# Four blocks of the attention output product, instead of two, computed between the heads up to their last depth block

## The chip, the cores and the metric

One core of one Trainium2 chip. The metric is the device time of the kernel in microseconds (us). The kernel before takes 2140.32 us, the median of three runs (2138.83 to 2141.16).

## What is computed

A two-layer trunk over 1024 positions of width 1024, all in float32: a gated linear recurrence and a squared-ReLU MLP, then chunked band attention with a learned relative bias and a second squared-ReLU MLP. The change lies in the attention layer and its output product:

```python
q = rmsnorm((rmsnorm(h, b_norm) @ b_w_q).reshape(bsz, s, N_HEADS, HEAD_DIM), b_q_norm)
o = chunk_band_attention(q, k_pad, v_pad, rel_bias)   # 16 heads of 64, chunks of 64, 8 chunks to the left
h = h + o @ b_w_o                                     # the output product
h = h + sqrelu_mlp(rmsnorm(h, mlp_norm), w_up, w_down)
```

## The kernel before

Activations lie transposed: 8 depth blocks of 128 features by 1024 positions, cut into two halves of 512 positions (`h` = 0, 1). To keep float32 accuracy every operand of a product is split into a high and a low part (an ACTIVATE makes the high part, a subtraction on VectorE or GpSimd the low part), and one 128x128 block by 512 columns takes three matmuls (`mm`, L334 to L336). Here such a triple is called a step. Weights come in pairs of raw 128x512 tiles, 256 KB each, and in the attention they are split at L297 (ScalarE) and L300 (VectorE) into tiles that the products read.

**The attention stage** (L1697 to L1720, in the trace from about 945 to 1455 us) is laid out by a planner written in the kernel (`Plan`, `Flag`, `Sema`): it simulates the engines with cost formulas and so fixes the order of the instructions on each queue. Two streams are interleaved.

- The *units* are the attention proper: 16 heads, two per depth block t, each in four units of 256 queries, so 64 units. A unit scores (L1556, L1557; VectorE adds the bias and takes the minimum at L1560, ScalarE the exponential at L1569, GpSimd scales at L1573), transposes the probabilities (L1581), splits them (L1589, L1591), and multiplies by the values into a bank `po` (L1608, L1609). After the second unit of a half, `leave` takes the result out (L1618, L1620). For t < 6 it is stored to DRAM (`od`); for t = 6 and 7 it is split at once by `halves` (L1632, L1634).
- The *filling* (`filling`, L1677) is dense matrix work: for t = 0 to 7 the projections of keys, queries and values (48 steps per t, 384 in all), and then `wo_steps`. This computes JP = 2 blocks of 128 output features of the output product over the first seven depth blocks only (the last one, t = 7, is not there yet): 2 blocks x 2 halves x 7 steps = 28 steps. The stored outputs are brought back during the last value projection and the first blocks (`reload`, L1638), six tiles per half, and split on ScalarE and GpSimd (L1632, L1634).

A unit may begin when the count of filling steps has reached its `due` value, and the filling may run at most SLACK = 14 steps past the next unit's due value. The due values are spread evenly over the filling:

```python
total = 8 * 6 * NF + 2 * JP * (NF - 1)        # 412 steps
cost = [1.0 if n.h else FR for n in units]    # FR = 0.9, sum 60.8
due = [START]                                 # START = 48
for c in cost:
    due.append(due[-1] + (total - START) * c / sum(cost))
```

When a block's seven steps are done, `Out.first` (L853 to L858) loads the residual `x2d` into a tile of the pool `sp` (tag s, NS = 10 tiles), adds the bank to it on VectorE (L857) and keeps the sum. The planner counts the addition but not the load. `weight` (L1477) hands out the next weight and starts the split of the one after it; the list `later` (L266 to L271) sets the order: the projections' weights, the first JP blocks of w_o, a tile `wl7` with the last depth block of all eight output blocks, then the remaining blocks of w_o.

**After the planned stage** (L1723 on) the order is set by the tile framework's scheduler, which may also place such instructions earlier, inside the stage, when their buffers are free. For the JP blocks the last depth block is one step per half; L1729 adds it to the kept sum, and `Out.last` stores the result, adds its square to the norm (L381, L387) and, for each finished pair of blocks, calls `combine` (L876 to L898), 11 VectorE and 8 ScalarE instructions that make the seven operands of the MLP's first product. `up_first` loads the first MLP weights. `whole` (L908) computes the other six blocks, 24 matmuls per block and half, each followed by `first` and `last`. Then `up_begin` (L1070) starts the MLP.

All DMAs are issued on SyncE's queue, in order; an issue waits there until its tile is free.

Of the kernel before, what the change touches and what calls it, by code (L numbers as in the profile page):

```python
# [40 lines left out]
C_ISSUE = 0.55  # L41
C_MOVE = 2.4
DEFER = 3
JP = 2
SC = (2.5, 5.0)
AHEAD = 1
ET = mybir.EngineType
# [110 lines left out]
def tile_yoco_rglru_chunk_attention(  # L158
# [108 lines left out]
    for t in range(NF):  # L267
        later += [(w_kv[t], g_kv, pool), (w_q[t], g_q, pool), (w_kv[NF + t], g_kv, pool)]
    later += [(w_o[j], None, WOE) for j in range(JP)]
    later.append((w_o[:, :, NF - 1, :].rearrange("j p m -> p j m"), None, dve))  # L270
    later += [(w_o[j], None, dve) for j in range(JP, NF)]  # L271
    loading, ready = [], []
# [36 lines left out]
    def next_w(late=False):  # L309
        while len(ready) < (1 if late else 2) and fetched[0] + len(loading) > 0:  # L310
            if not loading:
                if fetched[0] == len(wlist):
                    break
                fetch()
            prep()
        while len(loading) < AHEAD and fetched[0] < len(wlist):
            fetch()
        return ready.pop(0)
# [1337 lines left out]
    def wo_steps():  # L1656
        for j0 in range(0, JP, 2):
            js = range(j0, min(j0 + 2, JP))
            ws = []
            for _ in js:  # L1660
                w = yield from weight()
                ws.append(w)
            for h in range(2):
                for j, w in zip(js, ws):
                    ps = bank("pj")
                    for k in range(NF - 1):
                        if (h, j) == (0, js[-1]) and j0 == 0 and k < NF - 2:
                            plan.start(units[0].reload(k, 1))
                        yield split_o[k, h]
                        mm(ps, wparts(w, k), OS[k][h], k == 0, k == NF - 2)  # L1670
                        plan.pe(3 * H2)
                        if k == NF - 2:
                            o3.first(ps, j, h)
                            plan.use("dve", c_dve(H2))
                        yield None

    def filling():  # L1677
        for t in range(NF):
            projs.append(Proj(t))
            n = 0  # L1680
            for y in projs[t].steps():
                if y is None:
                    n += 1
                    if t == NF - 1 and 0 <= n - 5 * NF - 2 < NF - 2:
                        plan.start(units[0].reload(n - 5 * NF - 2, 0))
                yield y
        yield from wo_steps()

    fill = filling()
    total = 8 * 6 * NF + 2 * JP * (NF - 1)  # L1690
    cost = [1.0 if n.h else FR for n in units]
# [31 lines left out]
    wl7 = next_w()  # L1723
    for j in range(JP):
        for h in range(2):
# [74 lines left out]
```

## Time and profile before

| | |
|---|---|
| median of 3 runs | 2140.32 us |
| the profiled execution | 2141.76 us, span of the trace 2140.0 us |
| TensorE busy | 2092.7 us (98%), 9768 matmuls |
| VectorE / ScalarE / GpSimd busy | 1544.4 / 1106.4 / 577.2 us |
| chain that ended last, by engine | TensorE 86%, VectorE 6%, ScalarE 3%, DMA 2% |

The ends of matmuls are modelled and overlap the next one, so that a busy TensorE tells only that it did not wait; the time from one start to the next tells its pace. A row of a timeline gives the start, the duration, the engine, the line, the operation, the tile written and those read, the shape and the count, and in square brackets the engine's idle time before it and what ended it.

### The profile page before, as it was taken

What the parts mean: (1) busy time and instruction counts of PE and PEld (TensorE: products, weight loads), DVE (VectorE), ACT (ScalarE), POOL (GpSimd) and SP (SyncE); (2) the same over time, 40 slices, a digit from 0 to 9 for tenths busy, and PEclk for the clock granted to TensorE, in tenths of its full rate; (3) what the DMA queues carried; (4) which work ended last, traced back from release to release, by engine and by line L of the source; (5) the groups of instructions that cost most, each with busy time, mean ns of one, the idle gap of its engine ahead of it and who ended that gap; (6) DMA issues with size and microseconds to landing.
All of it is one profiled execution on the core that took longest, in us unless ns stands there. A gap on an engine that the chain in (4) does not pass through costs nothing.

```text
span 2140.0 us, 29346 instructions
## 1 busy us (share of the span) xinstructions
PE 2092.7 (98%) x9768; PEld 1732.8 (81%) x9768; DVE 1544.4 (72%) x2602; ACT 1106.4 (52%) x1965; POOL 577.2 (27%) x511
## 2 busy tenths in 40 slices
PE   7999899999999999999999999989999999999999
PEld 5788787888888888887888888878778888888887
DVE  7767768877777776747777877767787777777843
ACT  5777645444434544546666666764443444444631
POOL 0123202333310000127666666650133332000000
PEclk8999999999999999999999999999999999999999
DMA  4111334544469784534323332343364444987732
GB/s 139 35 50 50 107 116 153 182 158 153 149 231 314 240 259 131 161 121 109 86 75 97 91 91 83 87 151 123 103 215 148 155 156 170 332 262 242 244 109 94
DMA packets 174296, 319.21 MB, mean 149 GB/s; under 512 B 20544, under 2 KB 22592, under 8 KB 174144
## 3 DMA queue, kind: packets, MB, share of 16 engines
q1 hardware_dynamic: 174144, 317.33, 45.8%
q8 instruction: 77, 1.26, 0.2%
q14 instruction: 75, 0.61, 0.1%
HBM read 219.73 MB, written 78.64 MB: 139 GB/s over the span
## 4 chain that ended last, share of the span: by engine, by line
PE 86%; DVE 6%; ACT 3%; DMA 2%; issue 2%; SPq 1%; POOL 0%; DVEq 0%; POOLq 0%; ACTq 0%
PE pj L334 11%; PE pj L335 11%; PE pj L336 11%; PE tp L334 6%; PE tp L336 6%; PE tp L335 6%; PE sc L336 4%; PE sc L335 4%; PE sc L334 4%; PE p L335 4%; PE p L334 3%; PE p L336 3%; PE tp L1581 2%; PE po L1609 2%; PE po L1608 1%
## 5 line engine op out<-in xcount | busy, mean ns | idle before, releaser
L334 PE MATMUL pj<-h,wh 128*128 128x512 f32 x1198 | 481.5, 402 | 4.9 <-DVE s L1116 3.6
L335 PE MATMUL pj<-l,wh 128*128 128x512 f32 x1198 | 468.0, 391 | 0.7 <-POOL l L1634 0.7
L336 PE MATMUL pj<-h,wl 128*128 128x512 f32 x1198 | 467.9, 391 | 0.2
L1035 ACT ACTIVATE wh<-raw 128x512 fp32r<-128x512 f32 x349 | 219.1, 629 | 317.5 <-PE po L335 68.9
L1036 DVE TENSOR_TENSOR wl<-raw,wh 128x512 fp32r<-128x512 f32 x349 | 269.8, 775 | 100.3 <-ACT wh L1035 96.5
L336 PEld LDWEIGHTS pj<-h,wl 128*128 128x128 f32 x1198 | 225.2, 188 | 49.4 <-DVE wl L1036 1.0
L334 PEld LDWEIGHTS pj<-h,wh 128*128 128x128 f32 x1198 | 225.8, 189 | 48.5 <-DVE s L1116 4.4
L335 PEld LDWEIGHTS pj<-l,wh 128*128 128x128 f32 x1198 | 226.0, 189 | 38.8 <-POOL l L1634 1.4
L334 PE MATMUL tp<-h,wh 128*128 128x512 f32 x569 | 221.5, 389 | 0.0
L335 PE MATMUL tp<-l,wh 128*128 128x512 f32 x569 | 221.4, 389 | 0.0
L336 PE MATMUL tp<-h,wl 128*128 128x512 f32 x569 | 221.4, 389 | 0.0
L348 DVE TENSOR_TENSOR l<-raw,h 128x512 fp32r<-128x512 f32 x224 | 153.6, 692 | 30.1 <-ACT h L347 28.6
L347 ACT ACTIVATE h<-raw 128x512 fp32r<-128x512 f32 x224 | 137.5, 620 | 56.9 <-DMA raw<-hid 34.1
L335 PE MATMUL sc<-l,wh 128*128 128x512 f32 x425 | 165.8, 390 | 0.0
L336 PE MATMUL sc<-h,wl 128*128 128x512 f32 x425 | 165.7, 390 | 0.0
L334 PE MATMUL sc<-h,wh 128*128 128x512 f32 x425 | 165.4, 390 | 0.0
L334 PE MATMUL p<-h,wh 128*128 128x512 f32 x384 | 153.0, 398 | 11.3 <-ACT h L589 6.4
L1117 ACT ACTIVATE s<-s 128x512 f32<-128x512 f32 x125 | 78.4, 629 | 164.6 <-DVE s L1116 164.6
L1044 POOL TENSOR_TENSOR raw<-raw,raw 128x512 f32<-128x512 f32 x30 | 49.7, 1657 | 405.3 <-DVE wl L1036 398.3
L335 PE MATMUL p<-l,wh 128*128 128x512 f32 x384 | 152.5, 397 | 4.9 <-DVE l L592 2.4
L336 PE MATMUL p<-h,wl 128*128 128x512 f32 x384 | 151.3, 394 | 0.0
L334 PEld LDWEIGHTS tp<-h,wh 128*128 128x128 f32 x569 | 106.8, 188 | 22.4 <-ACT h L1632 0.3
(276 smaller groups left out, 4149.9 us busy)
## 6 DMA issues: line engine op xcount, KB each, us to landing
raw<-hid SPq DMA_DIRECT2D x224, 256.0 KB, 3.6
hid<-s SPq DMA_DIRECT2D x221, 256.0 KB, 2.1
raw<-in_w_down SPq DMA_DIRECT2D x192, 256.0 KB, 3.5
raw<-in_w_up SPq DMA_DIRECT2D x128, 256.0 KB, 2.6
s<-in_w_down SPq DMA_DIRECT2D x64, 256.0 KB, 4.3
raw<-in_w_in SPq DMA_DIRECT2D x32, 256.0 KB, 2.7
raw<-in_w_kv SPq DMA_DIRECT2D x32, 256.0 KB, 3.3
od<-ev SPq DMA_DIRECT2D x48, 128.0 KB, 2.2
```

What stands on the lines that cost most here:

```text
L334: pe.matmul(ps, lhsT=wh, rhs=xh, start=start, stop=False, skip_group_check=more)
L335: pe.matmul(ps, lhsT=wh, rhs=xl, start=False, stop=False, skip_group_check=more)
L336: pe.matmul(ps, lhsT=wl, rhs=xh, start=False, stop=stop, skip_group_check=more)
L347: act.activation(h, src, AF.Copy)
L348: dve.tensor_tensor(l, src, h.bitcast(F32), ALU.subtract)
L1035: act.activation(wh, raw, AF.Copy)
L1036: dve.tensor_tensor(wl, raw, wh.bitcast(F32), ALU.subtract)
L1044: pool.tensor_tensor(raw[A11], raw[A11], raw[A21], ALU.add)
L1117: act.activation(out, out, AF.Square)
L1581: pe.transpose(pt[:, g * P : (g + 1) * P], sc[:, (kb - kb0) * P : (kb - kb0 + 1) * P], ident)
L1608: pe.matmul(out, lhsT=st, rhs=ph[:, off : off + wid], start=x == 0 and y == 0, stop=False)
L1609: pe.matmul(out, lhsT=st, rhs=pl[:, off : off + wid], start=False, stop=y == final)
```

## The change

The constant JP becomes 4.

```diff
@@ -41,7 +41,7 @@
 C_ISSUE = 0.55
 C_MOVE = 2.4
 DEFER = 3
-JP = 2
+JP = 4
 SC = (2.5, 5.0)
 AHEAD = 1
```

What follows from it in the code: `later` lists four blocks of w_o ahead of `wl7` instead of two. `wo_steps` runs its outer loop twice (blocks 0 and 1, then 2 and 3), so that the filling has 384 + 56 = 440 steps and the due values are spread over 440. Only the first pair starts reloads. After the stage, the loop at L1724 runs over four blocks (eight steps, eight additions at L1729) and `whole` over the remaining four. The number of matmuls is the same.

## Rows read from the trace of the kernel before

**Rows 1.** The page's first part: each engine's busy time, its share of the span and its instructions.

```profile
PE 2092.7 (98%) x9768; PEld 1732.8 (81%) x9768; DVE 1544.4 (72%) x2602; ACT 1106.4 (52%) x1965; POOL 577.2 (27%) x511
```

**Rows 2.** Busy time of each engine in stretches of 20 us around the end of the attention stage (in brackets the instructions), then TensorE's granted clock as a share of 2.4 GHz, the busy share of the DMA engines and the bytes per second.

```profile
1360.00:1380.00 20.00, 20.00 (x120) 17.37 (x119) 16.93 (x49) 15.09 (x36) 14.39 (x17) 1.00 0.43 106
1380.00:1400.00 20.00, 19.11 (x108) 15.93 (x107) 17.41 (x34) 14.25 (x30) 7.98 (x9) 1.00 0.50 154
1400.00:1420.00 20.00, 16.30 (x85) 12.15 (x84) 14.61 (x40) 12.67 (x31) 13.90 (x15) 1.00 0.75 247
1420.00:1440.00 20.00, 17.89 (x100) 15.37 (x100) 11.65 (x37) 11.09 (x27) 11.06 (x12) 0.91 0.16 50
1440.00:1460.00 20.00, 19.73 (x114) 16.67 (x113) 15.40 (x34) 13.30 (x26) 3.50 (x4) 1.00 0.23 80
1480.00:1500.00 20.00, 20.00 (x90) 16.57 (x89) 13.33 (x21) 7.97 (x14) 0.00 (x0) 1.00 0.43 138
1540.00:1560.00 20.00, 17.41 (x75) 14.08 (x76) 17.35 (x26) 12.39 (x22) 8.33 (x6) 1.00 0.59 189
```

**Rows 3.** TensorE's timeline at the end of the stage: the instructions that it waited before.

```profile
1396.85 0.66 PE L1360 MATMUL tp<-ident,q 128*128 128x128 f32 x4 [0.79 <-DVE q L1355]
...
1403.00 0.50 PE L335 MATMUL pj<-l,wh 128*128 128x512 f32 x1 [0.72 <-POOL l L1634]
...
1405.93 0.39 PE L1609 MATMUL po<-pl,vs 128*128 128x256 f32 x1 [0.75 <-DVE pl L1591]
...
1411.81 0.39 PE L1556 MATMUL sc<-ev,ev 128*128 128x256 f32 x1 [1.72 <-DVE t L1560]
...
1417.39 0.55 PE L1581 MATMUL tp<-ident,sc 128*128 128x128 f32 x3 [0.44 <-POOL sc L1573]
...
1424.28 0.58 PE L1609 MATMUL po<-pl,vs 128*128 128x256 f32 x1 [1.87 <-DVE pl L1591]
```

**Rows 4.** VectorE's timeline in the same stretch: weight splits (L300) and the four additions of the residual (L857).

```profile
1399.97 1.83 DVE L300 TENSOR_TENSOR wl<-raw,wh 128x512 fp32r<-128x512 f32 x1
...
1403.72 1.83 DVE L300 TENSOR_TENSOR wl<-raw,wh 128x512 fp32r<-128x512 f32 x1 [1.07 <-ACT wh L297]
...
1408.89 0.69 DVE L300 TENSOR_TENSOR wl<-raw,wh 128x512 fp32r<-128x512 f32 x1 [0.47 <-ACT wh L297]
...
1410.79 0.69 DVE L857 TENSOR_TENSOR xr<-pj,s 128x512 f32<-128x512 f32 x1 [0.42 <-DMA s<-x2d]
...
1422.88 0.69 DVE L857 TENSOR_TENSOR xr<-pj,s 128x512 f32<-128x512 f32 x1 [3.58 <-DMA s<-x2d]
...
1436.57 0.68 DVE L857 TENSOR_TENSOR xr<-pj,s 128x512 f32<-128x512 f32 x1
...
1445.79 0.69 DVE L857 TENSOR_TENSOR xr<-pj,s 128x512 f32<-128x512 f32 x1 [0.72 <-PE pj L336]
```

**Rows 5.** SyncE's queue in the same stretch: DMA issues, merged; the duration runs from the first issue of a group to its last.

```profile
1400.07 3.16 SPq L243 DMA_DIRECT2D raw<-in_w_o  x6
1403.32 0.85 SPq L243 DMA_DIRECT2D raw<-in_w_up  x2
1404.26 0.63 SPq L243 DMA_DIRECT2D s<-x2d  x1
...
1410.03 8.91 SPq L243 DMA_DIRECT2D s<-od  x5
1419.90 17.70 SPq L243 DMA_DIRECT2D s<-x2d  x3
```

**Rows 6.** GpSimd's timeline: the splits of the reloaded outputs.

```profile
1395.77 7.17 POOL L1634 TENSOR_TENSOR l<-s,h 128x512 fp32r<-128x512 f32 x5 [10.61 <-ACT h L1632]
```

**Rows 7.** TensorE's timeline: the first and the last of 18 matmuls of the last value projection that follow each other without other work between.

```profile
1391.80 0.40 PE L334 MATMUL pj<-h,wh 128*128 128x512 f32 x1
...
1395.67 0.39 PE L336 MATMUL pj<-h,wl 128*128 128x512 f32 x1
```

**Rows 8.** VectorE's timeline after the stage: one of the additions of the last depth block (L1729); of each of the three `combine` calls in `whole`'s stretch the first and the last low part (L351); and residual additions (L857) between them.

```profile
1457.19 0.68 DVE L1729 TENSOR_TENSOR xr<-pj,xr 128x512 f32<-128x512 f32 x1
...
1458.61 0.75 DVE L351 SCALAR_TENSOR_TENSOR l<-xr,vec,h 128x512 fp32r<-128x512 f32 x1
...
1468.62 0.69 DVE L351 SCALAR_TENSOR_TENSOR l<-s,h 128x512 fp32r<-128x512 f32 x1 [0.76 <-ACT h L350]
1469.23 0.68 DVE L857 TENSOR_TENSOR xr<-tp,s 128x512 f32<-128x512 f32 x1
...
1482.06 0.69 DVE L857 TENSOR_TENSOR xr<-sc,s 128x512 f32<-128x512 f32 x1 [1.81 <-DMA s<-x2d]
1482.67 1.40 DVE L351 SCALAR_TENSOR_TENSOR l<-xr,vec,h 128x512 fp32r<-128x512 f32 x2
...
1491.82 0.68 DVE L351 SCALAR_TENSOR_TENSOR l<-s,h 128x512 fp32r<-128x512 f32 x1
...
1504.71 1.41 DVE L351 SCALAR_TENSOR_TENSOR l<-xr,vec,h 128x512 fp32r<-128x512 f32 x2
...
1513.04 0.68 DVE L351 SCALAR_TENSOR_TENSOR l<-s,h 128x512 fp32r<-128x512 f32 x1
...
1518.69 0.69 DVE L857 TENSOR_TENSOR xr<-sc,s 128x512 f32<-128x512 f32 x1 [3.18 <-PE sc L336]
```

**Rows 9.** SyncE's queue after the stage: four residual loads issued one behind the other.

```profile
1505.19 1.87 SPq L243 DMA_DIRECT2D s<-x2d  x4
```

## The prediction, made before the changed kernel was run

> **What bounds the kernel now.** I read the page's first part, the busy time by stretches of 20 us, the timelines of TensorE, VectorE, SyncE's queue and GpSimd between 1380 and 1460 us, and VectorE's timeline after it. TensorE is busy for 98% of the span [rows 1], so a change can give back only time in which it waits or runs slow. The stretches show where that is, near this change: 20.00 of 20 us are busy in the middle of the heads, then 19.11, 16.30, 17.89 and 19.73 in the four stretches from 1380 to 1460, and again 20.00 while `whole` runs [rows 2]. The four lack 0.89 + 3.70 + 2.11 + 0.27 = 6.97 us. In the third the granted clock is 0.91: if it is 1.2 GHz for a share x and 2.4 GHz for the rest, 1 - x/2 = 0.91, x = 0.18, so 3.6 us at half pace, which cost 1.8 us. The ceiling of what can come back here is 8.8 us.
>
> The cause is read from TensorE's six larger waits in that stretch [rows 3]: 0.79, 0.72, 0.75, 1.72, 0.44 and 1.87 us, 6.3 us together. The last two units' results come late from VectorE in the 1.72 and the 1.87, and both times VectorE stands at or just past an addition of the residual that waits for its load, 0.42 and 3.58 us [rows 4]. The units are tight behind each other because of the due values. They advance by (412 - 48)/60.8 = 5.99 steps per unit of cost, and a head costs 3.8, so the eight units of t = 7 begin to be due at step 48 + 53.2 x 5.99 = 366.5. Their queries need steps 353 to 368 and a norm behind them; the scores come only with the last value steps, near 384. Eight units then have 28 steps left between them, 3.5 each.
>
> **The change, part by part.** *Pace of the heads.* With 440 steps the spread is 392/60.8 = 6.45 per unit of cost. The first unit of t = 7 is due at 391.0, behind its projections, and the last of the 64 at 433.6, so 6.4 steps remain behind it (6.0 of 412 before). The eight units share 49 steps, about 6 each, as in the stretch with 20.00 busy [rows 2]. So each wait is priced on its own, from nothing to all of it:
> - 0.79 (value transposes with no head's work to fill): units of t = 6 now fall there. I take 0.8 back.
> - 0.72 (reloaded output not split yet): the six reloads per half and their GpSimd splits, 7.17/5 = 1.43 us each [rows 6], stay; two steps' matmuls still pass faster than one split. I take nothing back; the bounds are 0.7 back and 1.4 more.
> - 0.75, behind the weight splits: here eight splits of four weights follow each other, because the stage's last two weights are asked for at step 384 and what comes after the stage (six loads of w_o, four of the MLP's) is let in right behind [rows 4, 5]. With the change only two weights are split there and the rest moves to step 412, where the second pair is asked for. I take 0.5 back.
> - 1.72, the first residual addition behind that burst: its load is issued behind 8 x 256 KB and lands 6.5 us later (1404.26 to 1410.79) [rows 4, 5]. The first load now has half of that ahead; the fifth takes its place. I take 1.0 back.
> - 0.44 (GpSimd behind VectorE): 0.4 back.
> - 1.87 and the 1.8 us at half clock, the second addition: its load is issued only at 1419.90, because five reloads ahead of it on SyncE took 8.91 us for want of free tiles [rows 5]. A longer distance between units frees the tiles earlier in steps. I take 3.0 of 3.7 back.
>
> Together 5.7 us, between 0 and 8.8.
>
> *What it adds in the stage.* 2 blocks x 2 halves x 7 steps x 3 = 84 matmuls leave `whole`, where 90 in 20 us make 0.222 us each [rows 2], for the stage, where an undisturbed run has 17 intervals in 3.87 us, 0.228 [rows 7]: 84 x 0.006 = 0.5 us lost; above that, each pair of neighbours of another shape may cost more, up to 1 us. The four additions and loads of the residual move too. A residual load that lands in time costs no wait (the third and fourth additions [rows 4]); one that doesn't cost up to 1.87 plus the clock. The due steps put seven steps and one unit between two of the new ones, nothing but weights being queued ahead of them, so I take 0 with the upper bound as a rival below. The load that lets the addition wait holds the transposed probabilities' splits (L1591) behind it on VectorE, and TensorE waits for those.
>
> *The weights.* The splits of w_o's third block lay in the stage already; those of the fourth (two L300) are now needed there. Two L300 took 1.83 us beside GpSimd's splits, and 0.69 when it rested [rows 4, 6]: 2 x 1.14 = 2.3 us of VectorE at most, nothing at least. I take 0, as they are due when the reload splits are over. The Trainium skill, SBUF — State Buffer, "Who interferes with whom", says that a VectorE instruction with two SBUF inputs and a GpSimd one that reads SBUF exclude each other, the later one waiting for the whole of the earlier; the two rows at 1.83 agree. By that rule alone GpSimd's scaling of the probabilities would hold the moved splits as well, the 2.3 us would be paid, and the sum would be -2.2 instead of -4.5.
>
> *Behind the stage.* Four more additions at L1729, 0.68 us each [rows 8], 2.7 us of VectorE; four fewer sets in `whole`, 4 x 24 x 0.222 = 21.3 us of TensorE. Two calls of `combine` now stand back to back. Their lengths before are 1458.61 to 1469.3, 1482.67 to 1492.5 and 1504.71 to 1513.7: 10.7, 9.8 and 9.0 us [rows 8]. From the first one's start, VectorE needs 10.7 + 9.8, then four residual additions, then 9.0. If those four are issued as a group like the four loads at 1505.19 [rows 9], some 3 us; if they are spaced as between 1469.23 and 1482.06, where each load waited for the store before it, 12.8 us [rows 8]. So the third `combine` ends at 32.5 or 42.3. TensorE ended `whole` at about 1518.5, 59.9 us after that start, since the last addition waited for it 3.18 us [rows 8]; it now ends 21.3 sooner and has two to four more steps (0.7 us each) first: 40.0 to 41.4. VectorE is then in time, or late by 2 us plus the next two additions and the first splits of the fourth `combine`, 4.8 us in all, and `up_begin` has no cover for it (17.41 of 20 busy there [rows 2]). I take 0.7, nearer to the case of prefetched loads, since the order there is made by a scheduler that sees VectorE behind; the bounds are 0 and 4.8.
>
> Sum: -5.7 + 0.5 + 0.7 = -4.5 us. On the profiled execution that is 2141.76 - 4.5 = 2137.3 (its span of 2140.0 would be 2135.5, with 1.76 around it). This execution is 1.44 above the median, so on the median 2140.32 - 4.5 = 2135.8.
>
> **The rivals.**
> (1) *The stalls move to the second pair.* The burst of weights and MLP loads, let in at step 412, makes the fifth and sixth residual additions wait as the first and second did. For it: the burst depends on the last weights being asked for, which the change only moves. Against: no reloads stand in the queue there. Then 1.72 + 1.87 + 1.8 come back of what I counted as gained (4.0): -0.5 us, 2139.8. The rule of the Trainium skill named above (SBUF — State Buffer) would end near here too, at -2.2 us.
> (2) *VectorE is late behind the stage.* The two `combine` calls and spaced loads give the 4.8 us: -5.7 + 0.5 + 4.8 = -0.4, 2139.9.
> (3) *Slower: the new additions wait in the stage.* If the tiles of `sp` (ten) are short all through the last heads, each of the four new residual loads is issued late, VectorE stands 3.6 us and TensorE 1.87 each time, once or twice with the clock at half (1.8): 4 x 1.87 + 1.8 = 9.3 more, and the two old ones stay, so of the gain only 0.8 + 0.5 + 0.4 = 1.7 is left: 9.3 - 1.7 + 0.5 = +8, 2148. It decides from the point where a load lands later than about 1.7 us after VectorE reaches the addition (3.58 waited gave 1.87 idle). For it: two of four waited. Against: the third and fourth didn't, and three loads in 17.70 us [rows 5] show them issued ahead.
> (4) *It doesn't do what it says:* the planner could put the added steps behind the last unit. The due values exclude it; no chance is given.
>
> **How the numbers follow.** A measurement of this kernel can tell about 0.2%, 4.3 us, from no change. The forecast (waits mostly gone) has 0.46 and lies just past that line, at 2135.8; its own range is 2131.0 to 2138. Rivals 1 and 2 have 0.20 and 0.14 and end within 0.2%; rival 3 has 0.20, its milder forms (two or three waits) included, from about 2144.6 on. Faster 0.46, same 0.34, slower 0.20. The range begins at 2131.0 (the ceiling 8.8 with 0.5 lost and nothing behind the stage, and a little for small waits before) and reaches into the mild half of rival 3, 2145.5.
>
> **What would show it.** Right: in the last 80 us of the heads TensorE's busy time is near 20 per stretch, the clock stays at 1.00, and the eight L857 there wait for no DMA longer than 0.5 us. Wrong upstream: waits of 1.5 us or more before L1609 or L1556 behind an L857, at the second pair (rival 1) or at each one (rival 3). Wrong downstream: the third `combine` ends after `whole`'s last matmul, and TensorE is idle in `up_begin` for clearly more than before. The prediction falls if the time is above 2138 without one of these.

## The result, and the profile after

The changed kernel takes 2144.39 us (median of 20 runs, 2140.63 to 2146.56), the kernel before 2140.49 beside it (20 runs). The ratio is 1.0016, 95% interval 1.001 to 1.0022: slower by 2 to 5 us, where 4.5 us less was forecast. The profiled execution of after took 2144.29 us, its span is 2142.5 against 2140.0. One execution of e5 below took 3492.36 us at a mean granted clock of 0.556; e5's ratio leaves it out.

First the busy time of TensorE, VectorE and the rest in the same stretches as before, from the kernel after (columns as in [rows 2]):

```profile
1380.00:1400.00 20.00, 16.20 (x88) 13.58 (x86) 15.95 (x39) 12.97 (x30) 10.91 (x9) 0.91 0.59 185
1400.00:1420.00 20.00, 19.66 (x111) 16.49 (x110) 11.19 (x32) 11.03 (x26) 12.70 (x15) 1.00 0.33 104
1420.00:1440.00 20.00, 17.68 (x98) 14.99 (x97) 12.92 (x35) 11.17 (x25) 4.34 (x5) 0.91 0.41 131
1440.00:1460.00 20.00, 18.08 (x97) 14.78 (x96) 10.14 (x34) 8.63 (x20) 5.51 (x8) 1.00 0.21 68
1460.00:1480.00 20.00, 18.46 (x100) 15.31 (x99) 16.68 (x32) 12.71 (x25) 5.00 (x4) 1.00 0.33 120
```

1400 to 1420, the worst stretch of [rows 2] with 16.30, has 19.66 now: what the change was to repair is repaired. But 1380 to 1400 has fallen from 19.11 to 16.20, and behind 1420 three stretches lack about 2 us each. The granted clock is 0.91 in two of them, in one before. TensorE's timeline of after, the instructions that it waited before:

```profile
1387.58 0.66 PE L1360 MATMUL tp<-ident,q 128*128 128x128 f32 x4 [0.61 <-DVE q L1355]
1388.54 0.33 PE L1581 MATMUL tp<-ident,sc 128*128 128x128 f32 x1 [0.31 <-POOL sc L1573]
1389.32 0.98 PE L1581 MATMUL tp<-ident,sc 128*128 128x128 f32 x7 [0.45 <-POOL sc L1573]
1393.42 0.44 PE L1581 MATMUL tp<-ident,sc 128*128 128x128 f32 x2 [2.43 <-DVE pl L1591]
...
1428.65 0.39 PE L1609 MATMUL po<-pl,vs 128*128 128x256 f32 x1 [0.79 <-DVE pl L1591]
1431.48 0.68 PE L1581 MATMUL tp<-ident,sc 128*128 128x128 f32 x3 [1.54 <-POOL sc L1573]
1444.93 0.33 PE L1581 MATMUL tp<-ident,sc 128*128 128x128 f32 x1 [1.76 <-POOL sc L1573]
...
1472.01 0.50 PE L334 MATMUL po<-h,wh 128*128 128x512 f32 x1 [1.51 <-DVE o L1620]
```

All six waits of [rows 3] (6.3 us) are gone, and eight others (9.4 us) stand elsewhere, in three places: the **border**, where the last projection ends (3.80 us); the **second pair**, where the weights of blocks 2 and 3 are asked for (4.09); and the **tail**, where the last unit's result is needed (1.51). Over the attention from 995 us on and `whole`, with the smaller ones, TensorE waits 8.9 us before and 10.0 after.

*The border.* VectorE's timeline of after, ahead of the 2.43 us:

```profile
1388.98 0.82 DVE L300 TENSOR_TENSOR wl<-raw,wh 128x512 fp32r<-128x512 f32 x1 [0.88 <-ACT wh L297]
...
1392.08 0.69 DVE L300 TENSOR_TENSOR wl<-raw,wh 128x512 fp32r<-128x512 f32 x1 [1.10 <-ACT wh L297]
1392.68 0.69 DVE L1591 TENSOR_TENSOR pl<-tp,ph 128x512 fp32r<-128x512 f32 x1
```

And ScalarE's, ahead of the same wait:

```profile
1391.95 0.58 ACT L1589 ACTIVATE ph<-tp 128x512 fp32r<-128x512 f32 x1
```

VectorE stands 0.88 and 1.10 us for ScalarE's half of a weight split, and the split of the probabilities (L1591) that TensorE waits for is queued behind. But L1591 also reads what ScalarE's L1589 writes, and that ends only at 1392.53, 0.15 us before L1591 starts: most of the wait is ScalarE's queue itself. ScalarE is busy without a gap from 1386.17 to 1394.47 (reloaded outputs L1632, weights L297, value copies L1368, units L1569 and L1589).

*The second pair.* SyncE's queue, VectorE and GpSimd of after there:

```profile
1408.15 9.32 SPq L243 DMA_DIRECT2D s<-x2d  x3
1417.52 2.95 SPq L243 DMA_DIRECT2D raw<-in_w_o  x6
1430.12 7.56 SPq L243 DMA_DIRECT2D raw<-in_w_up  x4
...
1438.99 5.00 SPq L243 DMA_DIRECT2D s<-x2d  x3
```

```profile
1412.07 0.69 DVE L857 TENSOR_TENSOR xr<-pj,s 128x512 f32<-128x512 f32 x1 [1.16 <-DMA s<-x2d]
...
1428.90 1.20 DVE L300 TENSOR_TENSOR wl<-raw,wh 128x512 fp32r<-128x512 f32 x1
1430.02 0.15 DVE L1571 RECIPROCAL t<-t 128x1 f32<-128x1 f32 x1
1430.09 0.67 DVE L300 TENSOR_TENSOR wl<-raw,wh 128x512 fp32r<-128x512 f32 x1
...
1433.44 0.68 DVE L300 TENSOR_TENSOR wl<-raw,wh 128x512 fp32r<-128x512 f32 x1
...
1436.64 1.90 DVE L300 TENSOR_TENSOR wl<-raw,wh 128x512 fp32r<-128x512 f32 x3
1438.45 0.69 DVE L1036 TENSOR_TENSOR wl<-raw,wh 128x512 fp32r<-128x512 f32 x1
...
1442.95 0.69 DVE L857 TENSOR_TENSOR xr<-pj,s 128x512 f32<-128x512 f32 x1 [2.82 <-DMA s<-x2d]
...
1444.16 0.14 DVE L1571 RECIPROCAL t<-t 128x1 f32<-128x1 f32 x1
```

```profile
1428.76 0.80 POOL L1573 TENSOR_SCALAR sc<-sc,t 128x640 f32<-128x640 f32 x1 [5.93 <-DVE t L1571]
1430.26 1.16 POOL L1573 TENSOR_SCALAR sc<-sc,t 128x640 f32<-128x640 f32 x1 [0.71 <-DVE t L1571]
1439.22 1.30 POOL L1056 TENSOR_TENSOR raw<-raw,raw 128x512 f32<-128x512 f32 x1 [7.80 <-DVE wl L1036]
1440.60 1.29 POOL L1057 TENSOR_TENSOR raw<-raw,raw 128x512 f32<-128x512 f32 x1
...
1444.40 0.48 POOL L1573 TENSOR_SCALAR sc<-sc,t 128x256 f32<-128x256 f32 x1 [2.16 <-DVE t L1571]
```

The request for two weights is followed by six splits (L300) on VectorE and lets the MLP's preparation in (L1036, L1056, L1057). The fifth residual load is issued behind this burst, and its addition waits 2.82 us. VectorE's reciprocal for the next unit (L1571, 1444.16) is behind that, GpSimd's scaling waits for it, and TensorE for the scaling: the 1.76 us. So this is rival 1 in its place, with the fifth addition alone waiting; the sixth to eighth wait for no load. Of the eight, two wait for theirs (1.16 and 2.82), and behind the 1.16 TensorE waits 0.34 us (before L1608 at 1413.61, for VectorE's L1620).

### The profile page after: what moved, and what is told of

Read it like the earlier page. It is cut to its first block, busy times and chain, and to the rows that moved or that the text cites. A ratio compares the mean times of both kernels' runs of the same rounds, so it can differ in the third digit from the quotient of the medians.

```text
span 2142.5 us, 29345 instructions
## 1 busy us (share of the span) xinstructions
PE 2094.1 (98%) x9768; PEld 1735.9 (81%) x9768; DVE 1540.0 (72%) x2606; ACT 1105.6 (52%) x1965; POOL 583.0 (27%) x511
## 4 chain that ended last, share of the span: by engine, by line
PE 88%; DVE 5%; ACT 3%; issue 2%; DMA 1%; POOL 0%; SPq 0%; DVEq 0%; POOLq 0%; ACTq 0%
PE pj L334 12%; PE pj L335 12%; PE pj L336 12%; PE tp L334 6%; PE tp L336 6%; PE tp L335 6%; PE sc L334 4%; PE sc L336 4%; PE sc L335 4%; PE p L335 4%; PE p L336 3%; PE p L334 3%; PE tp L1581 2%; PE po L1609 1%; PE po L1608 1%
## 5 line engine op out<-in xcount | busy, mean ns | idle before, releaser
L334 PE MATMUL pj<-h,wh 128*128 128x512 f32 x1226 | 494.4, 403 | 3.8 <-DVE s L1116 3.6
L336 PE MATMUL pj<-h,wl 128*128 128x512 f32 x1226 | 480.2, 392 | 0.2
L335 PE MATMUL pj<-l,wh 128*128 128x512 f32 x1226 | 480.3, 392 | 0.0
L1036 DVE TENSOR_TENSOR wl<-raw,wh 128x512 fp32r<-128x512 f32 x349 | 270.1, 776 | 102.8 <-ACT wh L1035 99.0
L336 PEld LDWEIGHTS pj<-h,wl 128*128 128x128 f32 x1226 | 231.3, 189 | 50.9 <-DVE wl L1036 1.1
L334 PEld LDWEIGHTS pj<-h,wh 128*128 128x128 f32 x1226 | 231.8, 189 | 46.8 <-DVE s L1116 4.5
L335 PEld LDWEIGHTS pj<-l,wh 128*128 128x128 f32 x1226 | 232.1, 189 | 37.9
L334 PE MATMUL tp<-h,wh 128*128 128x512 f32 x562 | 218.7, 389 | 0.0
L334 PE MATMUL p<-h,wh 128*128 128x512 f32 x384 | 153.2, 399 | 11.1 <-ACT h L589 6.1
L336 PE MATMUL sc<-h,wl 128*128 128x512 f32 x411 | 159.9, 389 | 0.0
L335 PE MATMUL sc<-l,wh 128*128 128x512 f32 x411 | 159.9, 389 | 0.0
L334 PE MATMUL sc<-h,wh 128*128 128x512 f32 x411 | 159.9, 389 | 0.0
L294 POOL TENSOR_TENSOR raw<-raw,vec 128x512 f32<-128x512 f32 x48 | 56.4, 1176 | 262.4 <-DVE l L348 259.3
```

The lines of the kernel that those rows point to most:

```text
L294: pool.tensor_tensor(raw, raw, gains, ALU.mult)
L334: pe.matmul(ps, lhsT=wh, rhs=xh, start=start, stop=False, skip_group_check=more)
L335: pe.matmul(ps, lhsT=wh, rhs=xl, start=False, stop=False, skip_group_check=more)
L336: pe.matmul(ps, lhsT=wl, rhs=xh, start=False, stop=stop, skip_group_check=more)
L1036: dve.tensor_tensor(wl, raw, wh.bitcast(F32), ALU.subtract)
```

## The experiments

Each ran beside the kernel before on the same chip; the difference in us is (ratio - 1) x 2141. Not all ran on one chip (e1 to e4, e5 to e8, e9 with e10, and e11 with e12 each had their own), so compare the differences, and count each as uncertain by about 2 us.

| kernel | due over | blocks 2, 3 | residual | us | ratio, 95% interval | difference |
|---|---|---|---|---|---|---|
| after | 440 | pair | late | 2144.39 | 1.0016 [1.001, 1.0022] | +3.4 |
| e1 | 412 | pair | late | 2140.36 | 0.9996 [0.9987, 1.0005] | -0.9 |
| e2 | 440 | pair | early | 2143.18 | 1.001 [1.0002, 1.0019] | +2.1 |
| e3 | 440 | apart | late | 2138.70 | 0.9989 [0.998, 0.9998] | -2.4 |
| e4 | 440 | pair | late, other bank | 2144.26 | 1.002 [1.0011, 1.0029] | +4.3 |
| e5 | 412 | apart | late | 2137.84 | 0.9988 [0.9979, 0.9998] | -2.6 |
| e6 | 440 | two blocks only | late | 2143.77 | 1.0015 [1.0006, 1.0024] | +3.2 |
| e7 | 422 | apart | late | 2137.47 | 0.9981 [0.9972, 0.9989] | -4.1 |
| e8 | 412 | three blocks | late | 2138.22 | 0.9987 [0.9978, 0.9996] | -2.8 |
| e9 | 422 | pair | late | 2139.80 | 0.9993 [0.9984, 1.0002] | -1.5 |
| e10 | 422 | apart | early | 2135.45 | 0.9971 [0.9961, 0.9982] | -6.2 |
| e11 | 412 | two blocks only | early | 2138.25 | 0.9987 [0.9978, 0.9996] | -2.8 |
| e12 | 412 | apart | early | 2136.78 | 0.9983 [0.9974, 0.9992] | -3.6 |

Theory A: the later due values put units where the last projection ends, and that costs what the change gives. Theory B: the request for two weights in the middle of the units does. Theory C: the last bank makes the wait in the tail.

**e1: after, with the due values of before.**

```diff
-    total = 8 * 6 * NF + 2 * JP * (NF - 1)
+    total = 8 * 6 * NF + 2 * 2 * (NF - 1)
```

> Four blocks as in the changed kernel, but the due values of the units are spread over 412 steps as before the change, so that the last unit begins at step 406 and 28 of the 440 steps are left behind the heads. Theory A (the later heads are the cause: units of t = 6 are now in flight where the last projection ends, and their work stands on ScalarE and VectorE behind the reloads' and the weights' splits; waits of 2.43, 0.61, 0.45 and 0.31 us at 1387 to 1393 and a half-clock stretch): that group of waits goes back to what it was before the change, and the kernel is 3 to 5 us faster than the changed one, at or below the kernel before. Theory B (the second pair's requests at step 412 are the cause, waits of 0.79, 1.54 and 1.76 us and a half-clock stretch): the second pair now falls behind the last units, its waits shrink too, 2 to 4 us. Theory C (the bank po at the end, 1.51 us): nothing changes there, the gain stays under 1 us. If none of them holds: within 1 us of the changed kernel.

Measured 2140.36. The 2.43 us at the border and the wait in the tail are gone; three of the waits of [rows 3] are back, the last one at 1.71 in place of 1.87. From TensorE's timeline of e1:

```profile
1397.87 0.66 PE L1360 MATMUL tp<-ident,q 128*128 128x128 f32 x4 [0.78 <-DVE q L1355]
...
1404.02 0.50 PE L335 MATMUL pj<-l,wh 128*128 128x512 f32 x1 [0.72 <-POOL l L1634]
...
1422.57 0.38 PE L1609 MATMUL po<-pl,vs 128*128 128x256 f32 x1 [1.71 <-DVE pl L1591]
...
1443.21 0.38 PE L1609 MATMUL po<-pl,vs 128*128 128x256 f32 x1 [1.04 <-DVE pl L1591]
```

So the pace alone moves the time by 4.3 us (+3.4 to -0.9). It does not tell theory A from theory B: at this pace the second pair's waits shrink too, from 4.09 us to 1.04 and 0.59 at 1443 and 1444, as theory B had it.

**e6: before (two blocks), with the due values of four,** cut at 406 so that all units still begin.

```diff
-    total = 8 * 6 * NF + 2 * JP * (NF - 1)
+    total = 8 * 6 * NF + 2 * 4 * (NF - 1)
...
+    due = [min(x, 406.0) for x in due]
```

> The kernel before with two blocks, but the due values as in the changed kernel (spread over 440 steps, none above 406): the pace alone. Theory A: the waits at the border of the last projection (2.43 before the transposes of a unit, behind VectorE's L1591; 0.61 and 0.45) appear here too, at about 1387 to 1393, although no block was added, and the waits before L1609 and L1556 of two blocks stay; the last five units are crowded behind step 406, so the time is 2 to 6 us above the kernel before. Rival (the group comes from the third block's weights, asked for one pair earlier): the border shows 0.8 us at the value transposes as in the kernel before and no wait of 2 us.

Measured 2143.77. The border's row of after appears in a kernel that computes blocks 2 and 3 behind the stage. TensorE's timeline of e6:

```profile
1393.66 0.44 PE L1581 MATMUL tp<-ident,sc 128*128 128x128 f32 x2 [2.43 <-DVE pl L1591]
...
1446.66 0.39 PE L1608 MATMUL po<-ph,vs 128*128 128x256 f32 x1 [3.04 <-DVE o L1620]
```

The second row is the cost of crowding the last units, which after has not, so the time of e6 is not the border's price alone. With e1 it shows that the pace makes the border's waits: theory A's mechanism.

**e3: after, with blocks 2 and 3 one after the other.**

```diff
-        for j0 in range(0, JP, 2):
-            js = range(j0, min(j0 + 2, JP))
+        for js in [range(0, 2)] + [range(j, j + 1) for j in range(2, JP)]:
+            j0 = js[0]
```

> As the changed kernel, but blocks 2 and 3 follow one after the other (both halves of block 2, then both of block 3) instead of as a pair, so that their weights are asked for 14 steps apart and not at one step. Theory B in the form of the burst (six loads, six weight splits on ScalarE and VectorE between 1428 and 1438, and waits of 0.79 and 1.54 us with a half-clock stretch behind them): these waits go, 2 to 4 us faster than the changed kernel. Theories A and C: within 1 us of the changed kernel.

Measured 2138.70, below before. The three waits at the second pair are gone (20.00 of 20 us busy from 1420 to 1440); GpSimd's L1056 comes at 1454.18. Waits of 0.53, 0.45 and 0.70 us stand at 1443 to 1461 instead. The border's 2.42 and the tail's 1.5 us stay, but here the clock doesn't fall at the border. The gain on after is 5.8 us, more than the 2 to 4 that theory B asked for. So the pair's request is a second cause, and A alone falls.

**e2: after, with each residual loaded seven steps ahead into its kept tile.**

```diff
                     ps = bank("pj")
+                    xt = gf("xr")
+                    dma(xt, x2d[j, :, hs(h)])
+                    o3.XR[j][h] = xt
...
-                            o3.first(ps, j, h)
+                            dve.tensor_tensor(xt, ps, xt, ALU.add)
```

> As the changed kernel, but each block's residual is loaded seven steps earlier, straight into the tile that keeps the sum, so that no addition waits for its load. Theory B in the form that the prediction gave as rivals 1 and 3 (the residual's load lands late and holds VectorE: 2.82 us at 1442.95 and 1.16 us at 1412.07, TensorE 1.76 us at 1444.93): that wait goes, 1.5 to 3.5 us faster than the changed kernel, the upper end with one half-clock stretch less. Theories A and C: the waits at 1387 to 1393, 1428 to 1432 and 1472 stay, under 1 us gained.

Measured 2143.18. No addition waits for a load any more, yet TensorE's wait at the second pair stays. TensorE and GpSimd of e2:

```profile
1442.69 0.33 PE L1581 MATMUL tp<-ident,sc 128*128 128x128 f32 x1 [1.74 <-POOL sc L1573]
```

```profile
1439.55 1.29 POOL L1056 TENSOR_TENSOR raw<-raw,raw 128x512 f32<-128x512 f32 x1 [1.78 <-DVE wl L1036]
1440.92 1.26 POOL L1057 TENSOR_TENSOR raw<-raw,raw 128x512 f32<-128x512 f32 x1
1442.16 0.48 POOL L1573 TENSOR_SCALAR sc<-sc,t 128x256 f32<-128x256 f32 x1
```

With the load out of the way the scaling stands behind L1056 and L1057 on GpSimd, and is as late. The 1.3 us that e2 gains on after are within the noise. Two obstacles lay side by side, and taking one away showed the other.

**e4: after, with the product behind the last unit in another bank.**

```diff
-            ps = bank()
+            tag = "tp" if (j, h) == (3, 0) else None
+            ring[0] += tag is not None
+            ps = bank(tag)
```

> As the changed kernel, but the seventh of the eight last-depth steps behind the heads goes into a bank tp and not into po, which the last unit holds until its result is out (TensorE waited 1.51 us for that at 1472.01). Theory C (the eight steps now reach the bank po in the ring, the four of before did not): 1.5 us faster than the changed kernel, nothing else changes. Theories A and B: the same, since the order behind the heads has 20 us of work that could fill; within 0.7 us.

Measured 2144.26. The wait only changes its name, to 2.2 us before L334 behind ScalarE's L1632, the split of the last unit's result. Theory C falls. Every version at 412 or 422 steps is without this wait, so it belongs to the pace.

**e5 (412, apart), e7 (422, apart) and e9 (422, pair)** ask whether the two causes add. Their edits are e1's and e3's, and for 422

```diff
-    total = 8 * 6 * NF + 2 * JP * (NF - 1)
+    total = 422
```

> Four blocks, blocks 2 and 3 one after the other, and the due values over 412 steps: both changes that helped so far. Theory A and B add up (the later heads cost the group of waits at 1387 to 1393, the pair's requests at step 412 those at 1428 to 1445, each with a half-clock stretch): about 4 us faster than the changed kernel by the first and 6 by the second, of which the first brings back the waits of the kernel before (0.8, 0.7, 1.9 us), so 2 to 5 us below the kernel before, 2136 to 2139 us. Rival (with the old pace the second pair falls behind the last unit anyway, so that the requests cost nothing there): as the four blocks at the old pace alone, within 1 us of the kernel before.

> Four blocks, blocks 2 and 3 one after the other, due values over 422 steps: the units of t = 7 are due from step 375, the last one at 416, with 24 steps behind it. Theory A: the border's group of waits lies between the two paces, and the wait for the last unit's split (1.5 us behind L1620 in the changed kernel) is covered by the steps left: 1 to 3 us faster than the blocks one after the other at the pace of the changed kernel, 2136 to 2138 us. Rival: the pace matters little once the requests are apart: within 1 us of it, 2138.7.

> The kernel after with its due values spread over 422 steps in place of 440; blocks 2 and 3 stay a pair. Beside it stands the same pace with the two blocks one after the other, which took 2137.47 us (ratio 0.9981). Two causes, pace and pair: the border waits in front of L1581 behind VectorE's L1591 (2.4 us in the kernel after) are gone or smaller, but the group at step 412 (0.79, 1.54 and 1.76 us in the kernel after, with GpSimd's L1056 and L1057 and VectorE's L300 in it) stays, with a half-clock stretch near it; the time is 2139.5 to 2142. Pace alone: with the units earlier the pair's request disturbs nothing, the time is that of the version with separate blocks, 2137 to 2138.5. Pair alone: at least as slow as the kernel after, 2143 to 2145.

They don't add in full: from +3.4, the 4.3 of the pace and the 5.8 of the separate blocks would put e5 at -6.7, and it is at -2.6. Separate blocks bring 5.8 us at 440 (+3.4 to -2.4), 2.6 at 422 (-1.5 to -4.1) and 1.7 at 412 (-0.9 to -2.6). Each of these gains is uncertain by 2 to 3 us, so the last two can't be told apart, nor from nothing. But the pair at 422 (e9, 2139.80) ended where two causes put it, with waits of 0.54, 1.00 and 0.30 us at 1436 to 1440 and half clock from 1438.7, and e7 has none of these. At 422 steps the border has waits of its own, 1.27 and 2.06 us in e9 and 1.29 and 2.06 in e7.

**e8: three blocks, due values over 412** (`JP = 3`, and e1's line).

> Three blocks (the pair and a third one by itself), due values over 412 steps: half of what the change adds, without a second pair. Theory B (what costs is that two weights are asked for at one step in the middle of the heads, which also lets in what comes behind the stage): no burst here, 1 to 3 us faster than the kernel before. Rival (each added block costs by itself, in additions and loads): 0 to 2 us slower than the kernel before.

Measured 2138.22: a single third block at the old pace does as well as two (e5).

**e10, e12, e11: the early residual again, where the other obstacles are gone, and in before alone.** In e7 the second addition waited 4.67 us for its load, and TensorE 2.51 behind it. VectorE and TensorE of e7:

```profile
1418.27 0.69 DVE L857 TENSOR_TENSOR xr<-pj,s 128x512 f32<-128x512 f32 x1 [4.67 <-DMA s<-x2d]
```

```profile
1401.88 0.33 PE L1581 MATMUL tp<-ident,sc 128*128 128x128 f32 x1 [2.06 <-POOL sc L1573]
1419.67 0.39 PE L1609 MATMUL po<-pl,vs 128*128 128x256 f32 x1 [2.51 <-DVE pl L1591]
```

> The version with due values over 422 steps and blocks 2 and 3 one after the other (2137.47 us), and the residual of each of the eight results loaded seven steps ahead into its kept tile. There TensorE still waits 2.5 us before L1609 near 1416.9, behind VectorE's L1591. If that wait comes from the second residual addition standing at VectorE for its load, it goes, and the time is 2135 to 2136. If the weight splits and the reload's splits ahead on VectorE and GpSimd make it, as the 1.96 us that stayed when the residual came early in the kernel after, it stays at 1.5 us or more and the time is 2137 to 2138.5.

> The kernel after with due values over 412 steps, blocks 2 and 3 one after the other, and the residual loaded seven steps ahead. Without the early residual this took 2137.84 us, with one wait of 1.9 us before L1609 near 1422 and a half-clock stretch at 1425.8 (1.7 us). If the residual's load makes that wait, both go: 2134 to 2135.5, at or below the version at 422 steps (2135.45). If the pace of 422 steps is needed for it, the time is 2137 to 2138.5.

> The kernel before, with two blocks and due values over 412 steps; only the residual of each of the four results in the stage is loaded seven steps ahead into its kept tile. The kernel before waited 1.72 us at 1411.81 and 1.87 us at 1424.28, the latter with 1.8 us more at half clock, and VectorE stood 0.42 and 3.58 us for the load near them. If the loads make both waits, as the prediction counted them, the time is 3.5 to 5.4 us below the kernel before, 2136 to 2138. If the first comes from the weight splits alone (its 0.42 us speak for it), only the second goes: 2137.5 to 2139.5. If GpSimd's and VectorE's other work stands in its place, as when the residual came early in the kernel after: no change, 2140 to 2142.

e10 takes 2135.45, the best of all: it beats before by 6.2 us (interval 3.9 to 8.3) and after by more. All of TensorE's waits from 995 us to the end of `whole` in e10, in us in total, times and longest:

```profile
PE tp L1581 <- POOL sc L1573: 2.1, 1, 2.1
PE sc L1556 <- DVE t L1560: 1.5, 2, 1.3
PE pj L334 <- DVE xr L1676: 0.9, 1, 0.9
PE tp L1581 <- DVE pl L1591: 0.3, 1, 0.3
```

The 2.51 us is gone: that one was the load's. Most of what is left is the border's, 1.29 and 2.07 us. The same edit is worth 2.8 us in before (e11), where the 1.72 shrinks to 0.42 and the 1.87 with its half clock goes, while six waits of 0.17 to 0.45 come up; about 2 us in e7, and about 1 in e5 and in after; only the first of these is clear of its interval. By its time e11 lies in the case that only the second wait goes (2137.5 to 2139.5); by its rows both went, and the small ones took a part back. e12 (2136.78) fell between its two cases; by its rows the first came, for the wait near 1422 and the half clock behind it are gone. From e11 to e10 the four blocks, spaced and paced, bring 3.4 us, and from before to e7 4.1: near the forecast's 4.5, but not with the change as it was made, and the intervals of e11 and e10 overlap a little.

## Why the prediction was wrong

**What bounds the kernel** was read rightly as far as the rows show: the waits of TensorE and the stretches at half clock that came and went lie between 1380 and 1480 us and behind it. They don't add up to the time, though: from 995 us to `up_begin` after has 1.1 us more of waits and one more stretch at half clock (1.7 us lost), and yet it takes only 0.7 us longer. The rest makes up for some 2 us, and nothing read here shows where.

**Pace of the heads, the step that failed.** Its sum of 5.7 us was priced wait by wait, as if a wait that loses its cause left nothing behind.
- *0.79 (0.8 back).* The step had it that units of t = 6 fall there and fill the gap. They do fall there, but they are no filler: each needs ScalarE (L1569, L1589) and VectorE (L1591) just where the reloads and the weight splits already fill ScalarE. Instead of 0.8 back, 0.61 + 0.31 + 0.45 + 2.43 stand there, with 3.4 us at half clock behind them in the profiles of after and e6; in those of e2 and e3 the same waits have none. e1 removes the waits, e6 makes them.
- *0.75 and 1.72 (0.5 and 1.0 back).* Both are gone at their place. The halves of the burst that were moved to step 412 make 0.79, 1.54 and 1.76 there, and a second stretch at half clock. The text had this as rival 1, with 0.20; its argument against, that no reloads stand in the queue there, did not meet the burst of weights and MLP loads that the rival itself named, and GpSimd's L1056 and L1057 were in no term (e2, e3).
- *1.87 and the half clock (3.0 back).* Gone at their place, and made up for by the above.
- *0.72 and 0.44.* Both gone; 0 and 0.4 were taken.
- *The new residual loads (0, under what the change adds in the stage).* The reason given was that nothing but weights is queued ahead of them. The weights and the MLP's loads were enough: the fifth addition waits 2.82 us and TensorE 1.76 behind it; by e2, L1056 and L1057 alone would have made that wait.
- *The last unit.* "6.4 steps remain behind it", as many as before, was counted as no change; 1.51 us came up.

By the prediction's own signs it falls: the time is above 2138, and of the waits of 1.5 us or more only the 1.76 stands behind an L857, and that one before L1581. That 2144.39 lies below 2145.5, the upper end of what was thought possible, is luck, since that end came from rival 3.

**The clock makes up most of the sum.** The mean granted clock of after is 0.9922 (20 runs). For before it is 0.9937 beside e1 to e4 (32 runs), and 0.9933 to 0.9938 in the sets beside the other experiments. The difference, 0.0011 to 0.0016 of 2141 us, is 2.4 to 3.4 us of lost work, the larger part of the distance of the two medians (2144.39 - 2140.49 = 3.9). All four kernels slower than before, after, e2, e4 and e6, have the lowest clocks (0.9920 to 0.9928); the others have 0.9934 to 0.9939. The border's waits alone don't make a low clock: e3 keeps them and has 0.9939. Nor are the second pair's needed for one: e6 has no second pair and 0.9928. What lowers the clock was not taken apart further.

**The other terms.** 84 matmuls at the attention's pace: from 995 us to `up_begin` the next matmul starts 239.6 ns behind one of 512 columns before and 239.7 in after (means, without waits and half clock), some 0.3 us over 1470 of them, against 0.5. Behind the stage: after reaches the first matmul of `up_begin` 1.27 us later than before (1519.76 against 1518.49, of which 0.55 is there at 995), and keeps that distance to 1558, so VectorE delayed nothing and the cost of rival 2 did not come. Its condition did: the four residual additions between the second and the third `combine` are spaced by their loads (1497.65 to 1509.48), where the prediction leaned to loads issued as a group. The third `combine` ends at 1519.11, 41.3 us behind the first one's start (1477.77; 42.3 was reckoned for spaced loads), and only just ahead of `whole`'s last matmul (1519.54); the four additions that follow it come as a group. So 0.7 was near the truth by a margin of 0.4 us and not by its reason. VectorE of after:

```profile
1509.48 0.69 DVE L857 TENSOR_TENSOR xr<-pj,s 128x512 f32<-128x512 f32 x1 [1.80 <-DMA s<-x2d]
...
1518.42 0.69 DVE L351 SCALAR_TENSOR_TENSOR l<-s,h 128x512 fp32r<-128x512 f32 x1
1519.02 0.69 DVE L857 TENSOR_TENSOR xr<-tp,s 128x512 f32<-128x512 f32 x1
```

Rival 3 did not come either: the four new additions wait for one load, not four.

**The weights.** The two weight splits beside GpSimd's scaling took 1.20 and 0.67 us, where 0 was taken and 2 x 1.14 more was the bound. The Trainium skill's rule (SBUF — State Buffer, "Who interferes with whom") has the later one of the two wait for the earlier. The rows at 1428 to 1431 agree: the split that began during a scaling (1428.90, GpSimd until 1429.56) is the long one, and the scaling that began during a split (1430.26) took 1.16 in place of 0.80. That is 0.5 us of VectorE and 0.4 of GpSimd, and both lie on the chain that ends in a wait of TensorE: the long split, the reciprocal at 1430.02, the scaling until 1431.42, TensorE at 1431.48 after 1.54 us. So by these differences the term that was taken as 0 cost up to 0.9 us (an estimate). By the rule alone the prediction had 2.3.

**Left open.** In the profiled execution 1.2 of the 2.5 us are added behind 1558, by a half-clock stretch at 1564.9 that before's profile does not have, though both wait 1.8 us ahead of it (L334 behind L1116). Its share over many runs is in the mean clock and can't be told apart from the others'. Nor is it settled why the gains of pace and spacing don't add, and why 422 steps do better than 412 with separate blocks (e7 and e5, e10 and e12: intervals overlap).

## What to carry to other kernels

When a planner spreads work evenly, a longer filling moves every unit and not the last ones alone: look up what each unit lands on, engine by engine, ahead of counting a removed wait as gained. Ask for operands one at a time where the engines that prepare them also serve a latency chain, and issue a load on which an in-order engine may stand a whole group of steps ahead. Take the obstacles at one place away together, since each alone may only show the next.

## What the runs showed of the hardware

About the same wait of TensorE is followed by half clock in one execution and not in another. Stretches of 4 or 5 us (busy time, then the granted clock) behind the wait at the border, in after and in e3, and behind the 2.06 us that end at 1401.88 in e7 and at 1399.76 in e9:

```profile
1394.00:1398.00 4.00, 4.00 (x18) 3.67 (x18) 2.79 (x9) 1.12 (x3) 1.59 (x1) 0.57 0.59 179
```

```profile
1393.00:1398.00 5.00, 4.57 (x30) 4.18 (x31) 5.00 (x14) 2.79 (x6) 2.62 (x2) 1.00 0.59 180
```

```profile
1401.00:1406.00 5.00, 4.12 (x24) 3.44 (x25) 4.02 (x10) 2.58 (x6) 2.50 (x3) 1.00 0.36 113
```

```profile
1400.00:1405.00 5.00, 5.00 (x23) 4.21 (x23) 3.38 (x8) 1.87 (x5) 1.53 (x2) 0.66 0.18 53
```

The first and the last have stretches at 1.2 GHz, from 1394.2 and 1401.1, 3.4 us each; the middle two stay at 2.4 GHz. One such stretch costs 1.7 us, so a single profile can mistake it for an effect of the edit; the mean clock over all runs is the surer number.
